# Second half of a hybrid recurrent layer: LRU's three buffers as slots of RWKV's values

## The chip, the cores and the metric

The kernel runs on one core of one Trainium2 chip, as one launch. The time is the device time of that launch in microseconds (us), lower is better. Each kernel is run several times and the median counts. Engines are named as in the profile: PE (TensorE matmul), PEld (its weight load), DVE (VectorE), ACT (ScalarE), POOL (GpSimd) and SP (SyncE, which issues DMAs here). POOL issues DMAs too.

## What is computed

One layer (`DEPTH = 1`) of a recurrent trunk with `D_MODEL` 1024 is run on 1024 prompt tokens and on 8 single tokens that continue from given states. The reference, cut to what matters here:

```python
xn = _rmsnorm(x, norm1_g)
P = xn @ w_in                                   # one projection, columns split in three groups
o_r, S_r = _rwkv7(pm, ...)                      # A: 6 heads x 64, delta-rule matrix state
o_h, S_h = _hgrn2(ph, ...)                      # B: 6 heads x 64, gated matrix state
o_l, h_l, c_l = _rglru(pl, ...)                 # C: 256 channels, elementwise recurrence
mix = concatenate([o_r, o_h, o_l])
x = x + mix @ w_out
xn2 = _rmsnorm(x, norm2_g)
x = x + square(relu(xn2 @ mlp_w1)) @ mlp_w2
y = _rmsnorm(x, final_g)
# _rglru: causal convolution of width 4, two block-diagonal gates r and i,
# h_t = a_t h_{t-1} + sqrt(1 - a_t^2) (i_t x_t), output h * gelu(gate)
```

The outputs are y and the updated states of the three groups.

## The kernel before

**Tiles and halves.** Channels lie on the 128 partitions, tokens along the free dimension. The tokens are worked in two halves: `hf` 0 is tokens 0 to 511, `hf` 1 is tokens 512 to 1023 with the 8 sample tokens behind them. RWKV and HGRN have three channel tiles each (j = 0, 1, 2; two heads in a tile), LRU two (t = 0, 1). Dense products are made in three float32r matmuls for one (high times high, high times low, low times high), so an input column of 128 channels costs 24 matmuls of 512 tokens in the first half, and 24 of 256 and 24 of 264 in the second.

**Two kinds of work on PE.** PE's order is written by the program itself (`weave`, L106): a clock `now` that is modelled from matmul sizes picks the next piece. Six kinds of streams hold what depends on the recurrences: `rw_chain`, `rw_inverse` (twice), `rw_operands`, `rw_finish`, `hgrn` and `lru`. The filler holds the dense work: the input columns (`projections`, in the order of `ORDER`, L44), then the output projection of the first half (`out_proj(0)`), that of the second half and the start of the MLP. A stream that is ready goes first; the filler is taken in pieces of two matmuls while no stream is ready. A piece that yields a key waits until that key is set, with a modelled delay. The other engines are ordered by a scheduler with priorities. Every engine then runs its list strictly in order, with semaphores between the engines.

**Names in the rows.** A name ends in its tile and its half. `in2944_1_0` is input column 2944 in the second half, from its token 0; columns 2944 and 3200 are LRU's x and gate branch for t = 0, columns 3072 and 3328 the same for t = 1. `out3_0` is row tile 3 of the output projection of the first half, `out0_512` row tile 0 of the second half. `ch` is RWKV's chain over chunks, `W`/`Y` its triangular inverse, `gram`, `hS`, `ho`, `hoT` are HGRN's products, `hsrow`, `hso`, `hsq` those of HGRN's sample tokens, `lg` LRU's gates. `x_2_1` is tile 2 in the second half.

**Slots.** Values wait for their stream in slots. RWKV's r, k and v are tiles of tag `pm` (6 slots, `RPM`), three of them per tile j. HGRN's four inputs are tiles of tag `hpm` (8 slots, `HPM`), and LRU's x branch (`xb`) and gate branch (`gl`) are tiles of `hpm` as well. LRU has a third buffer `gq` of tag `lq` with one slot, and its convolution output `lxc` lies in a tag `xc` with one slot. A counter `free` stands in for the slots in the modelled order: `take("hpm")` (L398) makes the filler wait until one is free. HGRN gives its four back at the end of `hg_run`, in the second half behind `hg_sample`; LRU gives its two back at the end of `lru` (L1207); RWKV gives its three back when the second quarter of `rw_operands` is done.

In the second half the filler's order is w0 r0 h0 r1 r2 h1 h2 l0 l1. With h1 and h2 taken all 8 `hpm` slots are held, so l0 (t = 0) stands still until tile 1 of HGRN has been through `hg_sample`, whose last product is `hsq1`.

**`lru(t, hf)`** (L1144) does the GELU factor of the gate (L1155 to L1159, in `gq` and `gl`), the convolution (L1165 to L1170, from `xb` to `lxc`), the gate products `lg` on PE with a Tanh on ACT (L1187), then exponentials (L1192, L1193), a square root on ACT behind a table load (L1199), the scan (L1202), the sample tokens' update (L1204, L1205) and the output (L1206). It writes r over `xb` and i over `gq`, so that L1204 is the last reader of `xb`.

**`out_proj`** (L1231): residual inputs `xr` are brought by a DMA on POOL's queue (L1260) into slots of `pm`, and the squares for the second norm (`sq`, L1251) use `pm` slots too. Weights of a column are brought twice: by SP into `raw` (one slot), from which ACT makes `wh` (L291) and a negated copy in `wl` (L295), upon which POOL adds the weights again by an accumulating DMA (L296). `wh` and `wl` have two slots each, so that a column's weights can be made once the column two before it is done. For columns in a list `SOON` DVE subtracts instead (L293); row tiles 0 and 1 of `out_proj(0)` are in it.

Of the kernel before, what the change touches and what calls it, by code (L numbers as in the profile page):

```python
# [9 lines left out]
F32 = mybir.dt.float32  # L10
# [7 lines left out]
P = 128  # L18
# [6 lines left out]
CH = ((0, 512), (512, 256), (768, 264))  # L25
HT = 512
HW = HT + NB
# [9 lines left out]
RPM, HPM = 6, 8  # L37
# [15 lines left out]
def kernel(ctx: ExitStack, tc: tile.TileContext, i, o):  # L53
# [49 lines left out]
    def ev(key, delay=1.5):  # L103
        done[key] = now[0] + delay
# [91 lines left out]
    def vec(name, k, n=1):  # L196
        return vt[:, at[name] + k:at[name] + k + n]
# [121 lines left out]
    rwp = phase1.enter_context(tc.tile_pool(name="rwp", bufs=1))  # L319
    phase0 = ExitStack()  # L320
    hgp = phase0.enter_context(tc.tile_pool(name="hgp", bufs=1, side="right"))
# [74 lines left out]
    free = {"pm": RPM, "hpm": HPM}  # L396

    def take(tag):  # L398

        yield lambda: free[tag] > 0  # L400
        free[tag] -= 1
# [25 lines left out]
    def take_out(hf, out, pt):  # L427

        if hf == 0:
            V.tensor_tensor(out, pt, rb0, op=ALU.mult)  # L430
        else:
            S.copy(out, pt)
# [16 lines left out]

    bnd = const.tile([P, 11], F32, name="bnd")  # L450

    def shifted(hf, col, name, out, tag, bufs):

        k = col // P
        pr = rwp.tile([P, HT + 16], F32, tag="praw", name=f"praw_{name}", bufs=1)
        pm = rwp.tile([P, HW], F32, tag=tag, name=f"pm_{name}", bufs=bufs)

        def evac(pt, c0, n):
            take_out(hf, pr[:, c0:c0 + n], pt)

        yield from in_proj(hf, col, evac, shift=True)
        mu = vec("mu", k)
        n = HT if hf == 0 else HW
        G.tensor_scalar(pm[:, :n], pr[:, :n], omm[:, k:k + 1], 0.0, op0=ALU.mult, op1=ALU.add)
        V.scalar_tensor_tensor(pm[:, 1:HT], pr[:, 0:HT - 1], mu, pm[:, 1:HT], op0=ALU.mult, op1=ALU.add)
        if hf == 0:
            G.tensor_copy(bnd[:, k:k + 1], pr[:, HT - 1:HT])
        else:
            V.scalar_tensor_tensor(pm[:, 0:1], bnd[:, k:k + 1], mu, pm[:, 0:1], op0=ALU.mult, op1=ALU.add)
            V.scalar_tensor_tensor(pm[:, HT:HW], pr[:, HW:HW + NB], mu, pm[:, HT:HW], op0=ALU.mult, op1=ALU.add)  # L470
        out.append(pm)
# [416 lines left out]
    hgin, lruin = {}, {}  # L888

    def hp_tile(name):  # L890
        return hgp.tile([P, HW + 3], F32, tag="hpm", name=name, bufs=HPM)
# [237 lines left out]
    def lru_proj(t, hf):  # L1129
        if hf == 1:  # L1130
            yield ("LRU", t, 0)
        x = []
        for w in ("xb", "gl"):
            yield from take("hpm")
            x.append(hp_tile(f"l{w}{t}_{hf}"))
        xb, gl = x
        G.tensor_copy(xb[:, 0:3], lcar[:, t, 0:3])
        yield from in_proj(hf, COL_LX + t * P, lambda pt, c0, n: take_out(hf, xb[:, 3 + c0:3 + c0 + n], pt))

        yield from in_proj(hf, COL_LG + t * P, lambda pt, c0, n: take_out(hf, gl[:, c0:c0 + n], pt))  # L1140
        lruin[t, hf] = x
        ev(("lru", t, hf), 1.5)

    def lru(t, hf):  # L1144
        yield ("lru", t, hf)
        xb, gl = lruin[t, hf]
        gq = hgp.tile([P, HW], F32, tag="lq", name=f"lq{t}_{hf}", bufs=1)
        n = HT if hf == 0 else HW
        s0 = hf * HT

        def f(ap):
            return ap[:, 0:n]
# [38 lines left out]
        m = gq  # L1191
# [12 lines left out]
            V.tensor_tensor(hs[:, HT:HW], rt[:, HT:HW], cst[:, t, 24:32], op=ALU.mult)  # L1204
            V.tensor_tensor(hs[:, HT:HW], hs[:, HT:HW], m[:, HT:HW], op=ALU.add)  # L1205
        V.scalar_tensor_tensor(mix[6 + t][:, s0:s0 + n], f(gl), 0.5, f(hs), op0=ALU.mult, op1=ALU.mult)  # L1206
        free["hpm"] += 2  # L1207
        ev(("LRU", t, hf), 14.0)
        if hf == 0:
            V.tensor_copy(lcar[:, t, 3:4], hs[:, HT - 1:HT])  # L1210
# [20 lines left out]
    def out_proj(hf):  # L1231
# [12 lines left out]
        def evac(m, c0, cn, pt, xt):  # L1244
            xm = x2[m][:, c0:c0 + cn]
            V.tensor_tensor(xm, pt[:, :cn], xt, op=ALU.add)
            a = acc[c0][:, :cn]
            if m == 0:
                act(a, xm, AF.Square)
            else:  # L1250
                sq = rwp.tile([P, HW], F32, tag="pm", name=f"sq{m}_{c0}", bufs=RPM)  # L1251
                act(sq[:, :cn], xm, AF.Square)
                V.tensor_tensor(a, a, sq[:, :cn], op=ALU.add)
            if m == KT - 1:
                ev(("acc", c0), 2.5)

        def load(m):
            ws[m] = next_w(m + 1 < lead or m >= lead)
            xts[m] = rwp.tile([P, HW], F32, tag="pm", name=f"xr{m}_{hf}", bufs=RPM)
            nc.gpsimd.dma_start(xts[m][:, :n], i["xt"][m * P:(m + 1) * P, s0:s0 + n])  # L1260

        yield from split(KS[:6])
# [14 lines left out]
        xts = {}  # L1277
# [148 lines left out]
        return tuple(nhl(k, c0, n))  # L1426

    def norms():
        yield from norm2(*CH[0], lambda nm: rwp.tile([P, HW], F32, tag="pm", name=nm, bufs=RPM))
        for c in CH[1:]:  # L1430
            yield from norm2(*c, lambda nm: mlps[0].tile([P, 512], F32, tag="wl4", name=nm, bufs=2))

# [73 lines left out]
    for m in range(KT):  # L1506
        if m < 6:
            tag = ("wh8", "wl8", "raw8", "wl8", "wh8", "last")[m]
            w = (mlp if m == 5 else wpool).tile([P, 2, FB, P], F32R, tag=tag, name=f"w2_{m}", bufs=2 if tag[0] == "w" else 1)
# [94 lines left out]
```

## Time and profile before

| | |
|---|---|
| median of 3 runs | 1579.41 us (1573.84 to 1581.77) |
| the profiled execution's own time | 1583.56 us |
| its span | 1581.8 us (1.76 us lie around it) |
| PE busy | 1500.9 us, 95% of the span |
| DVE, ACT, POOL busy | 757.3, 665.3, 382.5 us |
| granted TensorE clock, mean | 0.972 |
| moved by DMA | 146.98 MB, 93 GB/s |

The page gives one profiled execution. Busy shares are averages over stages: the streams end at about 760 us of the span, and what follows is dense work alone. Three stretches of it, PE's busy time and granted clock: up to 600 us 559.61 of 599 us at 0.97; 600 to 800 us 175.59 of 200 us at 0.91; from 800 us on 765.72 of 780 us at 0.99. Starts of instructions are given in us from the start of the span. A matmul in float32 that is no float32r shows as two records, and a matmul's own duration is longer than the distance to the next, since they are pipelined: distances of starts are what a row of matmuls costs.

### The profile page before, as it was taken

The numbers are of one execution on the slowest core, as the hardware profiler recorded it, in microseconds if no ns is written. First come the engines' busy times: TensorE is split into PE (matmuls) and PEld (weight loads), VectorE is DVE, ScalarE is ACT, GpSimd is POOL, SyncE is SP. The second block draws the span as 40 slices with busy tenths as digits, with TensorE's granted clock in tenths as the row PEclk, the third lists the DMA queues.
The fourth block names the chain that finished last, engine by engine and source line by source line (L and its number), as shares of the span: only waits on it lengthen the run. The fifth ranks groups of instructions, "written<-read, shape, count | busy, mean of one in ns | idle before, by whom it ended". The sixth has DMA issues, their size and how long they took to land.

```text
span 1581.8 us, 31488 instructions
## 1 busy us (share of the span) xinstructions
PE 1500.9 (95%) x13112; PEld 1322.7 (84%) x13112; DVE 757.3 (48%) x1799; ACT 665.3 (42%) x1433; POOL 382.5 (24%) x531
## 2 busy tenths in 40 slices
PE   8989999999998899978999999999999999999997
PEld 6767777888898888866798899889898989988887
DVE  7777866756566665574555222222222222222224
ACT  4544656546544556255434324232332323233232
POOL 4553323224335324323312110101111010101011
PEclk9989999998999999799999999999999999999999
DMA  4334334344434334235442544535344454544242
GB/s 152 125 68 96 84 81 94 79 83 98 91 75 96 74 81 91 62 73 124 119 128 81 107 80 99 102 83 104 83 104 83 102 92 85 102 86 101 47 93 108
DMA packets 53086, 146.98 MB, mean 93 GB/s; under 512 B 6960, under 2 KB 7248, under 8 KB 52944
## 3 DMA queue, kind: packets, MB, share of 16 engines
q0 software_dynamic: 22976, 65.33, 24.9%
q1 hardware_dynamic: 29824, 79.61, 16.1%
q8 instruction: 103, 1.69, 0.5%
q14 instruction: 39, 0.32, 0.1%
q10 hardware_dynamic: 144, 0.04, 0.0%
HBM read 138.87 MB, written 6.07 MB: 92 GB/s over the span
## 4 chain that ended last, share of the span: by engine, by line
PE 72%; DVE 10%; issue 6%; ACT 5%; DMA 4%; POOL 2%; POOLq 0%; SPq 0%; DVEq 0%; ACTq 0%
PE up L76 22%; PE dn L76 19%; PE in L76 13%; PE out L76 4%; PE ch L76 2%; PE W L76 2%; PE Y L76 2%; PE sc L76 1%; PE gram L76 1%; DMA wl_out<-in_w_out 1%; DVE rq L1035 1%; PE ho L76 1%; DMA raw_in<-in_w_in 1%; DMA wl_w<-in_w 1%; ACT gsq L768 1%
## 5 line engine op out<-in xcount | busy, mean ns | idle before, releaser
L76 PE MATMUL in<-xl,wh_in 128*128 128x512 f32 (+3 forms) x648 | 223.4, 345 | 2.1 <-DVE xl L385 2.1
L76 PE MATMUL in<-xh,wh_in 128*128 128x512 f32 (+3 forms) x648 | 223.9, 345 | 0.0
L76 PE MATMUL dn<-hh,wl_w 128*128 128x264 f32 (+2 forms) x696 | 223.2, 321 | 0.3 <-DMA wl_w<-in_w 0.2
L76 PE MATMUL dn<-hh,wh_w 128*128 128x264 f32 (+2 forms) x696 | 222.8, 320 | 0.0
L76 PE MATMUL dn<-hl,wh_w 128*128 128x264 f32 (+2 forms) x696 | 222.7, 320 | 0.0
L76 PE MATMUL in<-xh,wl_in 128*128 128x512 f32 (+3 forms) x648 | 221.4, 342 | 0.5 <-DVE wl_in L293 0.3
L1492 DVE TENSOR_TENSOR mix<-mix,dn 128x512 f32<-128x512 f32 (+2 forms) x192 | 98.4, 512 | 243.4 <-PE dn L76 243.4
L296 POOL DMA_DIRECT2D wl_w<-in_w x86 | 75.2, 877 | 575.4 <-ACT hh L1422 305.9
L291 ACT ACTIVATE wh_w<-raw_w 128x512 fp32r<-128x512 f32 (+1 forms) x90 | 70.7, 785 | 281.6 <-PE dn L76 228.0
L1421 DVE SCALAR_TENSOR_TENSOR rl<-up,rl 128x512 f32<-128x512 f32 (+2 forms) x96 | 49.5, 516 | 204.5 <-ACT rl L1420 204.4
L76 PE MATMUL up<-nxh,wh_w 128*128 128x264 f32 (+1 forms) x512 | 145.9, 285 | 0.1
L76 PE MATMUL up<-nxl,wh_w 128*128 128x264 f32 (+1 forms) x512 | 145.0, 283 | 0.5 <-POOL nxl L1318 0.5
L76 PE MATMUL up<-nxh,wl_w 128*128 128x264 f32 (+1 forms) x512 | 145.3, 284 | 0.0
L76 PEld LDWEIGHTS dn<-hh,wl_w 128*128 128x128 f32 x696 | 130.8, 188 | 14.1 <-DMA wl_w<-in_w 4.4
L76 PEld LDWEIGHTS dn<-hl,wh_w 128*128 128x128 f32 x696 | 130.9, 188 | 10.1
L76 PEld LDWEIGHTS dn<-hh,wh_w 128*128 128x128 f32 x696 | 131.0, 188 | 9.3
L76 PEld LDWEIGHTS in<-xl,wh_in 128*128 128x128 f32 x648 | 127.4, 197 | 13.4 <-DVE xl L385 4.2
L76 PEld LDWEIGHTS in<-xh,wl_in 128*128 128x128 f32 x648 | 127.1, 196 | 11.1 <-issue 1.0
L76 PEld LDWEIGHTS in<-xh,wh_in 128*128 128x128 f32 x648 | 127.3, 196 | 10.6 <-issue 0.7
L1420 ACT ACTIVATE rl<-up 128x512 f32<-128x512 f32 (+2 forms) x96 | 43.3, 451 | 141.0 <-PE up L76 140.9
L76 PE MATMUL up<-nl,wh_w 128*128 128x512 f32 x256 | 101.5, 397 | 0.0
L76 PE MATMUL up<-nh,wl_w 128*128 128x512 f32 x256 | 101.5, 396 | 0.0
(461 smaller groups left out, 3328.3 us busy)
## 6 DMA issues: line engine op xcount, KB each, us to landing
raw_in<-in_w_in SPq DMA_DIRECT2D x53, 512.0 KB, 3.4
wl_in<-in_w_in POOLq DMA_DIRECT2D x43, 512.0 KB, 5.7
raw_w<-in_w SPq DMA_DIRECT2D x32, 512.0 KB, 3.5
raw_w<-in_w SPq DMA_DIRECT2D x64, 256.0 KB, 2.7
wl_w<-in_w POOLq DMA_DIRECT2D x58, 256.0 KB, 4.1
wl_w<-in_w POOLq DMA_DIRECT2D x28, 512.0 KB, 5.6
raw_out<-in_w_out SPq DMA_DIRECT2D x16, 512.0 KB, 3.5
out_y_prompt<-yt SPq DMA_DIRECT2D x16, 256.0 KB, 2.0
```

The costliest lines, as they stand in the source:

```text
L76: PE.matmul(out, lhsT, rhs, start=start, stop=stop)
L291: act(wh[:, ks], raw[:, ks], AF.Copy)
L296: G.dma_start(wl[:, ks], src[:, ks], accum_op=ALU.add)
L768: act(sq, raw[:, g * 64:(g + 1) * 64], AF.Square, bias=sums[:, 0, g:g + 1], accum_out=sums[:, 1, g:g + 1])
L1035: V.tensor_tensor(qp[g][hp, h, :], qef[hp, gc], q[hp, gc], op=ALU.mult)
L1420: act(rl[:, :n], pt[:, :n], AF.Relu)
L1421: V.scalar_tensor_tensor(rl[:, :n], pt[:, :n], 0.0, rl[:, :n], op0=ALU.max, op1=ALU.mult)
L1492: V.tensor_tensor(x2[m][:, c0:c0 + n], x2[m][:, c0:c0 + n], pt[:, :n], op=ALU.add)
```

## The change

In the second half LRU's buffers become tiles of `pm`, three instead of two: `gq` is taken together with `xb` and `gl` in `lru_proj`, and all three are given back at the end of `lru`. In the first half all three are `hpm` slots (three instead of two with the tag `lq` beside them). The tag `lq` is gone. `pm` tiles are 3 columns wider (523 instead of 520), since `xb` holds 3 tokens of carry. What sets the filler free for l0 in the second half is thus RWKV's tile 1 rather than HGRN's tile 1.

```diff
+    def pm_tile(name):
+        return rwp.tile([P, HW + 3], F32, tag="pm", name=name, bufs=RPM)
+
...
-        pm = rwp.tile([P, HW], F32, tag=tag, name=f"pm_{name}", bufs=bufs)
+        pm = pm_tile(f"pm_{name}") if tag == "pm" else rwp.tile([P, HW], F32, tag=tag, name=f"pm_{name}", bufs=bufs)
...
         x = []
-        for w in ("xb", "gl"):
-            yield from take("hpm")
-            x.append(hp_tile(f"l{w}{t}_{hf}"))
-        xb, gl = x
+
+        for w in ("xb", "gl", "gq"):
+            yield from take("pm" if hf else "hpm")
+            x.append((pm_tile if hf else hp_tile)(f"l{w}{t}_{hf}"))
+        xb, gl, gq = x
...
-        xb, gl = lruin[t, hf]
-        gq = hgp.tile([P, HW], F32, tag="lq", name=f"lq{t}_{hf}", bufs=1)
+        xb, gl, gq = lruin[t, hf]
...
-        free["hpm"] += 2
+        free["pm" if hf else "hpm"] += 3
...
-            xts[m] = rwp.tile([P, HW], F32, tag="pm", name=f"xr{m}_{hf}", bufs=RPM)
+            xts[m] = pm_tile(f"xr{m}_{hf}")
```

Lines behind L451 move on by 3 or 4 in the numbering (L1200 becomes L1203, L974 becomes L977). The number of instructions on each engine is the same. PE's order is the same up to the place shown first; from there to `out1_512`, a row tile of the second half's output projection, it differs. Buffer numbers stand behind the names.

PE before, the end of the last HGRN column (`in2816`) in the second half and what comes next:

```order
L76 MATMUL in2816_1_256_7845<-xl7_3310,wh_in2816_1_7576 128x264
L76 MATMUL in2816_1_256_7845<-xh7_3302,wl_in2816_1_7577 128x264
L76 MATMUL W2_2_1_1_7959<-xm_2_1_1_7737,sa_2_1_1_7735 64x64 x8
L76 MATMUL W2_2_1_1_7959<-vr_2_1_1_7462,kt_2_1_1_7461 64x64 x8
L76 MATMUL ho_1_1_7978<-vt_1_1_7200,att_1_1_7198 64x64 x16
```

PE after, the same place:

```order
L76 MATMUL in2816_1_256_7845<-xh7_3302,wl_in2816_1_7577 128x264
L76 MATMUL in2944_1_0_7969<-xh0_3295,wh_in2944_1_7797 128x256
L76 MATMUL in2944_1_0_7969<-xl0_3303,wh_in2944_1_7797 128x256
L76 MATMUL in2944_1_0_7969<-xh0_3295,wl_in2944_1_7798 128x256
L76 MATMUL in2944_1_0_7969<-xh1_3296,wh_in2944_1_7797 128x256
L76 MATMUL W2_2_1_1_7975<-xm_2_1_1_7737,sa_2_1_1_7735 64x64 x8
L76 MATMUL W2_2_1_1_7975<-vr_2_1_1_7462,kt_2_1_1_7461 64x64 x8
```

LRU's first column now begins here; before, only stream work stands from here on.

PE before, the last product of HGRN's tile 1 (`hsq1`), behind which the dense work goes on:

```order
L76 MATMUL gate_1_1_1_8170<-pm_xg1_3608,gup_162 128x256
L76 MATMUL hso1_8173<-hq1_1_6529,hsst1_8120 64x1 x16
L76 MATMUL W5_2_1_1_8194<-xm_2_1_1_7737,sa_2_1_1_7735 32x32 x8
L76 MATMUL hsq1_8205<-hssq1_8191,bones_84 128x8
L76 MATMUL in2944_1_0_8242<-xh0_3295,wh_in2944_1_7797 128x256
```

PE after, the same product:

```order
L76 MATMUL hso1_8266<-hq1_1_6529,hsst1_8170 64x1 x16
L76 MATMUL W5_2_1_1_8287<-xm_2_1_1_7737,sa_2_1_1_7735 32x32 x8
L76 MATMUL in3200_1_0_8209<-xl7_3310,wh_in3200_1_7963 128x256
L76 MATMUL in3200_1_0_8209<-xh7_3302,wl_in3200_1_7964 128x256
L76 MATMUL in3200_1_256_8301<-xh0_3295,wh_in3200_1_7963 128x264
L76 MATMUL in3200_1_256_8301<-xl0_3303,wh_in3200_1_7963 128x264
L76 MATMUL hsq1_8304<-hssq1_8284,bones_84 128x8
L76 MATMUL in3200_1_256_8301<-xh0_3295,wl_in3200_1_7964 128x264
```

At `hsq1` none of LRU's 192 input matmuls stood in front before, and 74 stand in front now. The same count at later products: at `hqk_2_1` 126 before and 190 now; at `hsq2`, the last stream product of all, 156 matmuls of `out_proj(0)` before (of 192), and all 192 with 10 of `out0_512` now.

DVE before, around HGRN's subtraction for level 3 of tile 2 (`kq3_2_1`); the end of LRU's t = 0 (L1200 to L1206) stands 28 rows further on, behind the subtraction for level 5:

```order
L1242 TENSOR_TENSOR ml2_8757<-mix2_71,mh2_8749 128x512
L1242 TENSOR_TENSOR ml3_8758<-mix3_72,mh3_8750 128x512
L992 COPY_PREDICATED att_2_1_8494<-cmask_88,gram1_0_2_1_8700 128x64x2
L974 TENSOR_TENSOR kq3_2_1_8787<-b_2_1_8491 128x512
L992 COPY_PREDICATED att_2_1_8494<-cmask_88,gram1_1_2_1_8701 128x64x2
```

DVE after, the same subtraction:

```order
L1249 TENSOR_TENSOR mix0_69<-out0_0_8694,xr0_0_8692 128x512
L727 TENSOR_TENSOR rh0_2_1_1_8799<-ch_2_1_1_8785,mv_2_1_1_7738 128x64
L1203 SCALAR_TENSOR_TENSOR lgq0_1_7960<-lgq0_1_7960,lxc0_1_8416 128x520
L731 COPY mv_2_1_1_7738<-ch_2_1_1_8785 128x64
L1205 SCALAR_TENSOR_TENSOR lxc0_1_8416<-lxb0_1_7958,lcar_202,lgq0_1_7960 128x512
L1207 TENSOR_TENSOR lxc0_1_8416<-lxb0_1_7958,lcst_206 128x8
L1159 TENSOR_SCALAR lgq1_1_8381<-lgq1_1_8381 128x520
L995 COPY_PREDICATED att_2_1_8579<-cmask_88,gram1_0_2_1_8835 128x64x2
L977 TENSOR_TENSOR kq3_2_1_8885<-b_2_1_8576 128x512
```

The end of LRU's t = 0 now stands in front of level 3 of HGRN and of a step of RWKV's chain (`mv`). On POOL the DMA of `xr1_0` moves from before `in2304` to between `kq2_2_1` and `kq3_2_1`: its slot is the one that `lxb0_1` had.

More of the change, by code (lines that the diff above doesn't have):

```diff
@@ L1250, in evac @@
             else:
-                sq = rwp.tile([P, HW], F32, tag="pm", name=f"sq{m}_{c0}", bufs=RPM)
+                sq = pm_tile(f"sq{m}_{c0}")
                 act(sq[:, :cn], xm, AF.Square)
@@ L1428, in norms @@
     def norms():
-        yield from norm2(*CH[0], lambda nm: rwp.tile([P, HW], F32, tag="pm", name=nm, bufs=RPM))
+        yield from norm2(*CH[0], pm_tile)
         for c in CH[1:]:
```

## The prediction

> **What bounds the kernel now.** I read the page first: the span, the busy time by engine and the shares of the chain that ended last.
>
> ```profile
> span 1581.8 us, 31488 instructions
> PE 1500.9 (95%) x13112; PEld 1322.7 (84%) x13112; DVE 757.3 (48%) x1799; ACT 665.3 (42%) x1433; POOL 382.5 (24%) x531
> PE 72%; DVE 10%; issue 6%; ACT 5%; DMA 4%; POOL 2%; POOLq 0%; SPq 0%; DVEq 0%; ACTq 0%
> ```
>
> PE is the bound: it is busy for 95% of the span, and 72% of the last chain runs on it. The change takes no matmul away. It can only give time where PE stands or where its clock is low, and behind the streams there is dense work alone, so that a microsecond won there should reach the end whole. So I looked for the place where the program's order departs, the end of the last HGRN column, and read PE's timeline there, at the last matmul of that column, the first stream product behind it, and the place where input columns go on.
>
> ```profile
> 620.40 0.28 PE L76 MATMUL in<-xh,wl_in 128*128 128x264 f32 x1
> 620.61 0.27 PE L76 MATMUL W<-xm,sa 64*64 64x64 f32 x2
> 643.01 0.36 PE L76 MATMUL hsq<-hssq,bones 128*128 128x8 f32 x1
> 643.23 0.56 PE L76 MATMUL in<-xh,wh_in 128*128 128x256 f32 x1
> ```
>
> From 620.6 to 643.2 us, 22.6 us, there is no input matmul: a hole in the dense work, with streams alone. Then a table of windows by stage, cut at the hole, at the changes of the granted clock and at LRU's gate products. Its columns are the stretch, its length, busy time and instructions of PE, PEld, DVE, ACT and POOL, the clock, the DMA share and GB/s.
>
> ```profile
> 620.60:632.20 11.60, 8.46 (x203) 7.56 (x202) 6.47 (x21) 8.67 (x42) 6.86 (x11) 1.00 0.54 124
> 632.20:643.20 11.00, 9.77 (x94) 7.53 (x95) 5.10 (x16) 0.65 (x3) 4.62 (x7) 0.50 0.06 25
> 643.20:652.70 9.50, 9.50 (x57) 9.21 (x58) 4.23 (x15) 0.61 (x2) 4.72 (x5) 0.50 0.10 29
> 652.70:665.40 12.70, 12.16 (x111) 10.63 (x111) 8.53 (x23) 3.29 (x5) 3.00 (x7) 1.00 0.46 104
> 665.40:686.60 21.20, 20.16 (x248) 19.00 (x247) 13.93 (x37) 15.03 (x41) 5.29 (x6) 1.00 0.31 76
> 686.60:713.10 26.50, 17.94 (x163) 13.05 (x161) 21.19 (x52) 14.59 (x24) 7.34 (x10) 0.89 0.29 71
> 713.10:770.60 57.50, 50.29 (x386) 39.36 (x385) 28.27 (x62) 28.37 (x66) 19.67 (x25) 0.96 0.59 144
> ```
>
> Two things show. PE is busy for 18.23 of the hole's 22.6 us, but the second half of that is at half clock, and so are the first 9.5 us of dense work behind it. And from 686.6 to 713.1 it is DVE that is busy (21.19 of 26.5), with PE at 17.94. Last, the view of waits, for the hole (617 to 646 us, the first two rows, its longest) and for the stage behind it (643 to 770 us, the other rows): who waits, for whom, total, times, longest.
>
> ```profile
> PE hoT L81 <- DVE gs L765: 1.6, 1, 1.6
> PE W L76 <- DVE rh L724: 1.4, 1, 1.4
> ...
> PE lg L76 <- DVE lxc L1168: 6.0, 1, 6.0
> PE out L76 <- DMA wl_out<-in_w_out: 3.1, 2, 2.0
> PE ho L76 <- DVE hst L1060: 1.8, 3, 0.9
> PE ho L76 <- ACT ad L1051: 1.1, 1, 1.1
> ```
>
> In the hole PE never waits longer than 1.6 us in a piece. The one long wait is at 711 us: LRU's gate products wait 6.0 us for the convolution on DVE.
>
> **The change part by part.** *The hole is filled.* With three slots of RWKV's values at hand, LRU's columns no longer wait for HGRN's tile 1, and 74 of their matmuls stand in front of `hsq1`. What fits in? The stream work of the hole costs 8.46 us where the clock was full and 9.77 at half clock, which I halve to 4.9: 13.35 us at full clock. That leaves 22.6 - 13.35 = 9.25 us for dense work, if the streams keep their pace. The check goes from the other side, by the distance of dense matmuls of the same column, at half clock and behind it at full clock:
>
> ```profile
> 650.64 0.42 PE L76 MATMUL in<-xh,wh_in 128*128 128x264 f32 x1
> 651.30 0.42 PE L76 MATMUL in<-xh,wh_in 128*128 128x264 f32 x1
> 652.87 0.29 PE L76 MATMUL in<-xh,wh_in 128*128 128x264 f32 x1
> 654.60 0.28 PE L76 MATMUL in<-xh,wl_in 128*128 128x264 f32 x1
> ```
>
> From 652.87 to 654.60 lie 14 steps, 0.124 us each; from 650.64 to 651.30 three, 0.22 each. 74 x 0.124 = 9.15 us, which is what is free. I take 9.25. The bound from below is what stands idle with the clock as it is: 22.6 - 18.23 = 4.4 us. **First term: -9.25 (at least -4.4).**
>
> *The half clock behind the hole.* The 9.5 us from 643.2 to 652.7 are dense work at 0.50. If it is the thin work of the hole that brings the clock down, then with dense matmuls among the stream products it stays up, and the same work takes 4.75. **Second term: -4.75 (between 0 and -4.75).** The row for it is the table's second: PE was busy for 8.46 of 11.6 us with small products of heads, and then the clock fell. [...]
>
> *The weights in the hole.* LRU's first column has to have its weights when the hole begins. The accumulating DMAs that finish them are issued by POOL here; behind them is the page's row for such DMAs (count, size, median us from issue to landing):
>
> ```profile
> 614.77 0.92 POOL L296 DMA_DIRECT2D wl_in<-in_w_in  x1 [1.92 <-ACT hg L911]
> 624.10 0.91 POOL L296 DMA_DIRECT2D wl_in<-in_w_in  x1 [2.83 <-ACT wl_in L295]
> wl_in<-in_w_in POOLq DMA_DIRECT2D x43, 512.0 KB, 5.7
> ```
>
> The first lands at about 614.77 + 5.7 = 620.5, just as it is wanted, the second at 629.8, where half of the hole's dense work is still the first column's. So they are covered; were they not, the wait would be the 5.7 us of one landing at most. Term: 0.
>
> *LRU's end moves ahead of HGRN's level 3 on DVE.* This is what the change adds. DVE before has the subtraction for `kq3_2_1` at 686.28, and LRU's end for t = 0 far behind it; now that end (from the scan's factor to the sample tokens) stands in front of the subtraction, of the copies of `gram1` and of RWKV's `mv`, all of which are queued behind it, and PE's next HGRN products behind these. The first instruction of that end waits for ACT:
>
> ```profile
> 686.28 0.73 DVE L974 TENSOR_TENSOR kq<-b 128x512 f32<-128x512 f32 x1
> 687.54 0.72 POOL L979 TENSOR_TENSOR kq<-kq,hf 128x256 f32<-128x256 f32 x1 [4.72 <-ACT kq L975]
> 698.52 1.05 ACT L291 ACTIVATE wh_out<-raw_out 128x1024 fp32r<-128x1024 f32 x1
> 702.35 0.64 ACT L1199 ACTIVATE lq<-lq 128x520 f32<-128x520 f32 x1
> 703.02 0.70 DVE L1200 SCALAR_TENSOR_TENSOR lq<-lq,lxc 128x520 f32<-128x520 f32 x1 [2.50 <-ACT lq L1199]
> 705.36 0.14 DVE L1204 TENSOR_TENSOR lxc<-lxb,lcst 128x8 f32<-128x8 f32 x1
> ```
>
> DVE waits 2.50 us there for the square root, which stands on ACT behind a weight copy and a table load. Before, that wait held little; now HGRN's tile 2 and RWKV's chain are behind it. I take those 2.5 us whole. From the good side the cost is 0: LRU as a whole is earlier, and the wait may be over. From the bad side it is the distance from where level 3 was to where LRU's end was, 705.36 + 0.14 - 686.28 = 19.2 us. I lean to the near row, because LRU's columns come forward by some 14 us and take their end with them. **Third term: +2.5 (0 to +19.2).**
>
> *The DMA of `xr1`.* It takes the slot of `lxb0_1` and so waits, on POOL's queue, for the same end of LRU; `kq3_2_1`'s product on POOL, at 687.54 before, stands behind it. Its releaser is the one of the third term, and what is queued behind it is held on DVE by it too: nothing on top, or with LRU late, the same 19.2.
>
> *The rest.* `lxb` and `lgl` in wider tiles, the first half's third `hpm` slot, and the slot that `lq` leaves change no instruction of the first half nor its order: 0. LRU's t = 1 has its gate buffer in the slot that `xr0` uses as well, and its convolution still has the one `lxc` slot: no wait for these shows before, and I take 0 here and price it as a rival.
>
> *The sum.* -9.25 - 4.75 + 2.5 = -11.5 us. The profiled execution's own time is 1583.56 us, 4.15 above the median of 1579.41: 1572.1 against the one, **1567.9 us** on the median, which I predict. A check from the far end: suppose nothing at all makes the streams end earlier, and `hsq2` stays where it is.
>
> ```profile
> 758.23 0.28 PE L76 MATMUL hsq<-hssq,bones 128*128 128x8 f32 x2
> 758.37 0.48 PE L76 MATMUL out<-mh,wh_out 128*128 128x512 f32 x1
> 761.24 0.39 PE L76 MATMUL out<-mh,wh_out 128*128 128x512 f32 x1
> 763.83 0.50 PE L76 MATMUL out<-mh,wl_out 128*128 128x512 f32 x1 [1.96 <-DMA wl_out<-in_w_out]
> 770.59 0.28 PE L76 MATMUL out<-mh,wh_out 128*128 128x256 f32 x1
> ```
>
> Then 36 matmuls of `out_proj(0)` at 0.23 us (12 steps between the second and the third row, 2.87 us) and 10 of `out0_512` at about 0.12 lie ahead of it that lay behind: 8.3 + 1.2 = 9.5 us, and 11.5 with the wait of 1.96 for weights among them. The same size comes out of both ends.
>
> **The rivals.**
> *The clock stays low.* What brings the clock down may be something other than the hole's thin work. Then the second term is gone and the first is its lower bound: -4.4, 1575.0 us. For it: the dense 9.5 us from 643.2 ran at 0.50 too, so that dense work alone did not bring the clock back at once. Against it: the other long stretches, 652.7 to 686.6, are dense among streams and at 1.00. [...]
>
> *LRU's second tile waits.* PE's 6.0 us for the convolution come back for t = 1, whose convolution stands behind t = 0's output and whose first square stands behind `out0`: -11.5 + 6.0 = -5.5, 1573.9 us. For it: DVE is the fullest engine there (21.19 of 26.5). Against it: the view of waits has that wait once, not twice.
>
> *Slower.* LRU's end keeps its own time, because its gates wait for DVE and ACT rather than for its columns. Level 3 of tile 2 then goes from 686.28 to 705.5, 19.2 us later, in place of the 2.5, and the end of the streams with it: -14.0 + 19.2 = +5.2. PE runs out of dense work meanwhile, since all of `out_proj(0)` lies ahead, and a second hole costs a second stretch at half clock, 4.75: +9.95, 1589.4 us. It decides once L1207 (L1204 before) ends later than 686.28 + 14.0 = 700.3 us, which is 5.2 before it ended. For it: the 6.0 us wait and the full DVE just there. Against it: the columns that LRU waits for were the last thing to come, from 643.2 on.
>
> *More than the hole.* What the order makes wait goes too, since streams and dense work now lie beside each other up to the end: the 6.0, the 3.1 for weights, 1.8 and 1.1 of `ho`, 12.0 in all, and no third term: -14.0 - 12.0 = -26.0, 1553.4 us. For it: each of these has dense work that could stand ahead of it. Against it: the order puts LRU's gates as close behind their columns as before.
>
> That the change does nothing is excluded by PE's order, in which LRU's columns stand in the hole.
>
> **How the numbers follow.** The forecast has 0.48; its own range, with the second term between its bounds and the third between 0 and 2.5, goes from -14.0 to -6.75, 1565.4 to 1572.7 us. The low clock has 0.10, the second tile's wait 0.10, slower 0.17, more than the hole 0.15. About 0.5%, 7.9 us, is what a measurement of this kernel can tell from no change, so faster begins below 1571.5: the forecast but for 0.03, and the case of more, 0.60. Slower begins above 1587.3: the slower rival where the second half clock comes with it, 0.14. Within lie the low clock, the second tile, 0.03 of the forecast and 0.03 of the slower case without the clock, 0.26. The range goes from 1554 to 1584, near the bottom of the case of more and short of the slower rival with its clock; it leaves out 0.05 below and 0.14 above.
>
> **What would show it.** First term: input matmuls from 620.6 on, 70 or so ahead of `hsq1`, and `hsq1` still near 643. Second: a granted clock near 1.00 from 632 to 653. Together: the first dense matmul of `out0`, at 686.6 before, near 673. Third: DVE's wait at L1203 for ACT at 2.5 us or less, and level 3's subtraction (L977) no later than 700. The sum: `out0_512`, at 770.6 before, near 759. The forecast is wrong if the clock is low in the same place, if level 3 comes later than 700.3, or if PE shows a wait of over 5 us at 620 to 640 for weights.

## The result, and the profile after

The changed kernel took 1569.05 us in the median of 6 runs, the kernel before 1578.24 us in 6: a ratio of 0.995, with a 95% interval from 0.9926 to 0.9973. That is 9.2 us faster; timed again beside the experiments it was 10.6 us faster (0.9942, 0.9922 to 0.9963). The profiled execution took 1567.39 us with a span of 1565.4. Ratios and intervals leave out one run, of a variant below (the one with 1567.25 us in the median), that took 2032.54 us at a granted clock of 0.65.

The two profiled executions lie 16.2 us apart, more than the medians, and the first thing is to find where. The last matmul of the last HGRN column (`in2816`), where the two orders part, starts at 620.40 us before and at 617.41 after: 3.0 us were won ahead of the place at which the change begins, in code whose order is the same. They are no part of the change: two further profiles of the kernel before have that matmul at 617.90 and 617.02. From there to the last matmul of `out7_768` (826.06 and 811.23) it is 205.7 against 193.8 us, 11.8 less, and 1.3 more come behind. So the stage between these two matmuls is what has to be compared, and its times below count from the end of `in2816`.

The page after, with the busy times and the chain that ended last:

```profile
span 1565.4 us, 31493 instructions
PE 1484.2 (95%) x13112; PEld 1309.8 (84%) x13112; DVE 759.7 (49%) x1799; ACT 664.3 (42%) x1433; POOL 382.2 (24%) x531
...
PE 68%; DVE 12%; ACT 6%; DMA 6%; issue 5%; POOL 2%; SPq 0%; POOLq 0%; ACTq 0%; DVEq 0%
```

PE has the same number of matmuls and is busy for 16.7 us less over the whole span: much of what this pair of profiles shows is matmuls that ran at a higher clock (0.983 granted in the mean over the span, 0.972 before). In the stage itself PE is busy for 172.3 us and was for 179.8, 7.5 less, and idle for 4.4 less. PE's timeline after at the places that the prediction named:

```profile
617.41 0.28 PE L76 MATMUL in<-xh,wl_in 128*128 128x264 f32 x1
617.54 0.28 PE L76 MATMUL in<-xh,wh_in 128*128 128x256 f32 x1
...
642.31 0.39 PE L76 MATMUL hsq<-hssq,bones 128*128 128x8 f32 x2
...
669.02 0.39 PE L76 MATMUL out<-mh,wh_out 128*128 128x512 f32 x1
...
752.17 0.28 PE L76 MATMUL out<-mh,wh_out 128*128 128x256 f32 x1
...
811.23 0.28 PE L76 MATMUL out<-mh,wl_out 128*128 128x264 f32 x1
```

LRU's first column follows upon `in2816` at once. `out0` begins 51.6 us behind the end of `in2816`, 66.2 before; `out0_512` 134.8 against 150.2. The windows at the same four times as before, with the work 3.0 us further on in them:

```profile
620.60:632.20 11.60, 11.15 (x191) 10.45 (x188) 5.12 (x16) 5.97 (x38) 6.97 (x9) 1.00 0.48 118
632.20:643.20 11.00, 10.33 (x135) 8.87 (x133) 8.62 (x23) 3.44 (x7) 5.17 (x7) 1.00 0.51 121
643.20:652.70 9.50, 9.50 (x88) 8.84 (x87) 6.52 (x19) 3.82 (x6) 6.34 (x8) 1.00 0.44 103
652.70:665.40 12.70, 12.45 (x115) 11.09 (x113) 9.74 (x27) 7.49 (x16) 3.58 (x5) 1.00 0.41 111
```

The clock is at 1.00 in all four, and PE is idle for 1.1 of the first 22.6 us where it was idle for 4.4. A long wait of LRU's gates behind the hole is still there (643 to 757 us):

```profile
PE lg L76 <- DVE lxc L1171: 5.1, 1, 5.1
PE out L76 <- DMA wl_out<-in_w_out: 4.9, 2, 2.7
PE ch L76 <- DVE rh L727: 2.4, 1, 2.4
PE hsq L76 <- DVE hssq L1118: 1.7, 1, 1.7
```

And on DVE, the end of LRU's t = 0 with level 3 of HGRN's tile 2 behind it:

```profile
681.00 0.70 DVE L1203 SCALAR_TENSOR_TENSOR lgq<-lgq,lxc 128x520 f32<-128x520 f32 x1 [1.05 <-ACT lgq L1202]
...
682.94 0.14 DVE L1207 TENSOR_TENSOR lxc<-lxb,lcst 128x8 f32<-128x8 f32 x1
...
683.57 0.72 DVE L977 TENSOR_TENSOR kq<-b 128x512 f32<-128x512 f32 x1
```

DVE waits 1.05 us for the square root, and LRU's end is over at 65.7 us behind `in2816`, where it was over at 85.1 before.

### The profile page after: what moved, and what is told of

The parts are those of the page before. It is cut to its first block, busy times and chain, and to the rows that moved or that the text cites. A ratio compares the mean times of both kernels' runs of the same rounds, so it can differ in the third digit from the quotient of the medians.

```text
span 1565.4 us, 31493 instructions
## 1 busy us (share of the span) xinstructions
PE 1484.2 (95%) x13112; PEld 1309.8 (84%) x13112; DVE 759.7 (49%) x1799; ACT 664.3 (42%) x1433; POOL 382.2 (24%) x531
## 4 chain that ended last, share of the span: by engine, by line
PE 68%; DVE 12%; ACT 6%; DMA 6%; issue 5%; POOL 2%; SPq 0%; POOLq 0%; ACTq 0%; DVEq 0%
PE up L76 21%; PE dn L76 20%; PE in L76 12%; PE ch L76 2%; PE out L76 2%; PE W L76 2%; PE Y L76 2%; DMA raw_w<-in_w 1%; PE gram L76 1%; DMA wl_out<-in_w_out 1%; PE sc L76 1%; DMA wl_in<-in_w_in 1%; DMA raw_out<-in_w_out 1%; DMA mix<-in_xt 1%; PE ho L76 1%
## 5 line engine op out<-in xcount | busy, mean ns | idle before, releaser
L76 PE MATMUL in<-xl,wh_in 128*128 128x512 f32 (+3 forms) x648 | 218.8, 338 | 1.9 <-DVE xl L385 1.7
L76 PE MATMUL in<-xh,wh_in 128*128 128x512 f32 (+3 forms) x648 | 219.0, 338 | 0.0
L76 PEld LDWEIGHTS dn<-hh,wl_w 128*128 128x128 f32 x696 | 130.8, 188 | 13.7 <-DMA wl_w<-in_w 3.9
L76 PEld LDWEIGHTS in<-xl,wh_in 128*128 128x128 f32 x648 | 123.7, 191 | 13.0 <-DVE xl L385 4.2
L76 PEld LDWEIGHTS in<-xh,wl_in 128*128 128x128 f32 x648 | 123.6, 191 | 12.5 <-DVE wl_in L293 1.9
L76 PEld LDWEIGHTS in<-xh,wh_in 128*128 128x128 f32 x648 | 123.5, 191 | 10.4 <-issue 0.7
L76 PE MATMUL up<-nh,wh_w 128*128 128x512 f32 x256 | 101.5, 396 | 0.0
```

Of the source, the lines that this page charges most:

```text
L76: PE.matmul(out, lhsT, rhs, start=start, stop=stop)
```

## The experiments

Two theories were at stake. The one: the hole is filled with dense work, and the clock stays up with it. The other: something else that came with the new slots (a gate buffer of its own for each LRU tile, less waiting for slots) moves LRU along. Later a third question came up, whether the gain is partly given back where the streams end. In each experiment the ratio is to the kernel before, run beside it on the same chip.

**The slots without the early start.**

```diff
         if hf == 1:
             yield ("LRU", t, 0)
         x = []
+        if hf == 1:
+            yield lambda: free["hpm"] > 0
```

> The changed kernel with all its slots, but in the second half LRU's first column is held back until HGRN's tile 1 has given its slots back, so that PE's order is that of the kernel before, row for row. Theory (the hole is filled, and the clock with it): nothing is left of the gain, 1578 us within 4, ratio 0.998 to 1.002, with 22.6 us free of input matmuls and a stretch of 10 to 20 us at half clock in them. Rival (the slots themselves: a gate buffer of its own for each LRU tile lets LRU flow): half of the gain or more is kept, 1573.5 us or less.

Measured: 1583.15 us against 1580.23, ratio 1.0022 (1.0004 to 1.0041). Nothing of the gain is left, and the slots alone are rather a small loss. The hole and its half clock are back. The two rows are the stretch from the end of `in2816` to `out0`, and from there to the end of the stage; the columns are length, then PE's busy time, and the clock is the first number behind the five engines:

```profile
616.80:683.20 66.40, 60.09 (x709) 53.95 (x708) 38.65 (x112) 28.51 (x93) 25.28 (x33) 0.85 0.32 78
683.20:826.30 143.10, 120.61 (x950) 103.31 (x949) 81.94 (x168) 62.80 (x122) 37.66 (x47) 0.94 0.43 112
```

A clock of 0.85 over 66.4 us means 20 us at half clock. Here and before these come in one piece of 20.5 us that begins in the hole. The rival falls: it is the early start that carries the gain. What LRU's earlier end alone is worth in it was not tried.

**Matmuls of no use in the hole.** The product is read by nobody; nothing of the computation is left out.

```diff
         if hf == 1:
             yield ("LRU", t, 0)
         x = []
+        if (t, hf) == (0, 1):
+            pd = ps("big", "dum")
+            while free["hpm"] == 0:
+                for _ in range(2):
+                    mm(pd[:, 0:264], xh[0][:, 0:P], xh[1][:, 0:264])
+                yield 0.0
```

> The kernel before, with 72 matmuls of 264 columns put in the hole whose product nobody reads; LRU's columns start where they did. It does no useful work in the hole and only keeps PE busy. Theory: the granted clock is at 1.00 through the hole and behind it, which is worth the second term alone, 4.75 us: 1573.5 us, range 1571 to 1576. Rival (the clock is all of the gain): as the changed kernel, 1569 us. Rival (the half clock doesn't come from thin work): the clock stays at 0.50, the 72 cost 0.22 us each, 15.8 us against 4.4 us idle, and the time is 1578 to 1590 us.

Measured: 1578.31 us against 1580.23, ratio 0.9985 (0.997 to 1.0), a gain of some 2 us and not 4.75.

```profile
619.20:681.20 62.00, 60.03 (x780) 55.29 (x780) 38.20 (x111) 28.44 (x93) 24.85 (x33) 1.00 0.33 79
681.20:820.30 139.10, 118.11 (x949) 101.36 (x948) 81.47 (x168) 62.91 (x122) 37.39 (x46) 0.96 0.44 113
```

The clock is at 1.00 over the whole first stretch, where before had 0.85, so that the theory on its cause holds in this profile: with useless matmuls in the hole it stays up. The stretch is 4.2 us shorter than before (62.0 against 66.2), close to the second term. Further profiles of the kernel before, below, give a reason why the median shows only half of that.

**Two thirds of the dose.** Only the x branch of t = 0 starts early.

```diff
-            yield from take("pm" if hf else "hpm")
-            x.append((pm_tile if hf else hp_tile)(f"l{w}{t}_{hf}"))
+            tg = "pm" if hf and (t or w == "xb") else "hpm"
+            if (t, hf, w) == (0, 1, "gl"):
+                yield from in_proj(hf, COL_LX + t * P, lambda pt, c0, n: take_out(hf, x[0][:, 3 + c0:3 + c0 + n], pt))
+            yield from take(tg)
+            x.append((pm_tile if tg == "pm" else hp_tile)(f"l{w}{t}_{hf}"))
...
-        free["pm" if hf else "hpm"] += 3
+        if (t, hf) == (0, 1):
+            free["pm"] += 1
+            free["hpm"] += 2
+        else:
+            free["pm" if hf else "hpm"] += 3
```

> The changed kernel, but for t = 0 only the x branch takes a slot of RWKV's values; gate branch and gate buffer wait for HGRN's slots. 48 input matmuls instead of 74 stand in front of the last product of HGRN's tile 1. Theory: 48 x 0.124 = 5.95 us of the first term's 9.25; if the clock stays up as well, 9/14 of the gain or a little more is kept, some 6 to 7 us: 1571.5 us, range 1569.5 to 1573.5. Rival (a threshold: the clock falls as soon as the hole has any part without dense work): the first term's part alone and less, 3 us: 1575 us.

Measured: 1580.33 us, ratio 1.0011 (0.9995 to 1.0027). Both expectations missed: there is no gain at all. The windows are the filled part, the part that is left of the hole, and the dense work behind it:

```profile
619.20:634.30 15.10, 14.18 (x250) 13.13 (x249) 8.19 (x23) 9.13 (x44) 7.56 (x10) 1.00 0.41 95
634.30:644.70 10.40, 7.21 (x97) 5.56 (x95) 9.66 (x24) 2.72 (x5) 5.32 (x6) 0.80 0.54 128
644.70:654.30 9.60, 9.56 (x56) 9.27 (x57) 4.20 (x15) 0.72 (x3) 4.93 (x4) 0.50 0.10 27
```

A hole of 10.4 us is left; PE is idle for 3.2 of it, and the clock falls in it (0.80 in the mean) and stays down through the dense work behind (0.50), 13.7 us in all. So in this profile a shorter hole has the same consequence. That is the threshold rival's mechanism, at a price higher than it named. Not all of it is settled: in this one profile the stage takes 200.8 us, which is 4.8 less than in the profile of before, and over 12 executions nothing of that is left. PE also waits 7.6 us for the convolution of t = 1 here, 5.1 in the changed kernel, so that the clock need not be all of it.

**The changed kernel once more.**

> The changed kernel once more, for a second profile and a narrower interval beside the others. Theory: 1569 us within 2.5, the clock at 1.00 from 632 to 653 us, and part of the gain given back between the last product of HGRN's tile 2 and the third row tile of the second half's output projection, 2 to 4 us, because the streams' end moved less than the dense work. Rival (that part is where half-clock stretches happened to fall in the one profile): it is within 1 us of 0 in this profile.

Measured: 1569.67 us against 1580.23, ratio 0.9942 (0.9922 to 0.9963). The two rows are again the stretch to `out0` and the rest of the stage:

```profile
617.30:670.80 53.50, 50.90 (x638) 46.21 (x637) 36.33 (x99) 26.91 (x85) 23.32 (x31) 0.97 0.40 97
670.80:813.40 142.60, 123.48 (x1021) 106.90 (x1021) 86.98 (x181) 64.79 (x131) 39.08 (x49) 0.93 0.43 112
```

The stage takes 196.1 us, 9.6 less than before, where 12.7 had been won up to `out0`: 3.1 are given back behind it, of the size expected, though over a longer stretch than the expectation named. The clock is not at 1.00 all the way: 3.4 us at half clock came at 642.5.

**Is the part given back to be had?** Three kernels tried what might hold the streams' end. The first puts LRU's gates for t = 1 behind HGRN's last level; the second gives t = 1 a convolution slot of its own; the third, a control, makes the first edit in the kernel before.

```diff
             gram(l, *kq)
             kq = nx
+            ev(("gram", l, n), 0.0)
...
         yield D39
+        if (t, hf) == (1, 1):
+            yield ("gram", 5, "2_1")
```

> The changed kernel, but PE takes LRU's gate products for t = 1 only behind HGRN's last level (gram5) of tile 2, and dense work stands in their place. Theory (part of the gain is given back because PE's wait of 5.1 us for LRU's second convolution now stands ahead of HGRN's levels 3 to 5, so that the streams end as late as before): level 3 comes about 6 us earlier, the last stream product 3 us or more, and some 3 us come back: 1566.5 us, range 1565 to 1568. Rival (the dense work alone sets the end): as the changed kernel, 1569.7 us within 1.5. Rival (LRU's second tile is late for the output projection instead): 1572 us.

Measured: 1567.25 us against 1576.13, ratio 0.9941 (0.9921 to 0.9961): as the changed kernel. The time lies in the theory's range, but here the kernel before took 1576.13 us beside it where it took 1580.23 earlier, so that only the ratios can be compared. In its profile the wait for the convolution is gone, and yet level 3's subtraction comes 71.6 us behind `in2816` and the last stream product 141.5, no earlier than in the changed kernel's profiles (66.2 to 69.4, 139.0 to 142.5).

```diff
-        xc = hgp.tile([P, HW], F32, tag="xc", name=f"lxc{t}_{hf}", bufs=1)
+        xc = hgp.tile([P, HW], F32, tag="xcb" if (t, hf) == (1, 1) else "xc", name=f"lxc{t}_{hf}", bufs=1)
```

> The changed kernel with a slot of its own for the convolution output of LRU's t = 1 in the second half; PE's order is that of the changed kernel, and DVE makes the second convolution ahead of HGRN's tile 2 levels. Theory: PE's wait of 5.1 us for it goes (under 1 us is left), HGRN's levels 3 to 5 follow sooner, and 3 to 5 us are won: 1566 us. Rival (the wait goes but DVE's convolution pushes HGRN's levels 2 and 3 back by the same 4 us): as the changed kernel, 1569.7 us within 1.5.

Measured: 1567.99 us, ratio 0.9939 (0.9913 to 0.9965): as the changed kernel, and the last stream product comes at 141.9 us. The wait of 5.1 us for the convolution is gone from PE's list of waits, and the largest one for the gates is another:

```profile
PE out L76 <- DMA wl_out<-in_w_out: 5.2, 2, 2.7
PE lg L76 <- ACT lxb L1190: 2.5, 1, 2.5
```

> The kernel before with LRU's gate products for t = 1 behind HGRN's last level, as in the run of the changed kernel with the gates late. Here 36 matmuls of the first half's output projection still lie behind the last stream product, so that the streams' end isn't the bound. Theory: within 2 us of the kernel before, 1578 to 1582, though the longest wait there (6.0 us) shrinks or goes. Rival (that wait costs its 6.0 us wherever it stands): 1574 to 1575 us.

Measured: 1578.06 us against 1576.13, ratio 1.0009 (0.9987 to 1.003): nothing, as expected. But the edit did little here: the wait has only shrunk to 4.7 us, and the gates come 85.9 us behind `in2816`, where two further profiles of before have them at 83.9 and 84.0. So this control says little about the wait. In the changed kernel, taken away in two ways, it is worth nothing that these intervals show. A gain of up to 3 us isn't excluded by them, but none was found. My theory that the streams' end gives the 3 us back, through this wait, isn't borne out.

**More slots.** `RPM` is 7 instead of 6, and so `xr1` no longer waits for LRU's end.

```diff
-RPM, HPM = 6, 8
+RPM, HPM = 7, 8
```

> The changed kernel with 7 slots for RWKV's values instead of 6, so that the residual inputs of the output projection and LRU's second gate buffer wait less for LRU's buffers. PE's order is the same. Theory (the DMA of xr1 behind LRU's end costs nothing, as I took it): 1569.7 us within 1.5. Rival (POOL's queue held by that DMA delays HGRN's level 3): 2 to 4 us faster, 1566 to 1567.5.

Measured: 1568.3 us against 1576.13, ratio 0.9949 (0.9929 to 0.9969): no gain, although in the changed kernel POOL stands still for 3.10 us for that DMA:

```profile
683.38 0.57 POOL L1263 DMA_DIRECT2D xr<-in_xt  x1 [3.10 <-DVE lxc L1207]
```

**The kernel before, twice more.** The control above held a surprise in its profile: in the hole, in an order that is before's up to there, the clock was at half for 3.4 us and not for 20.5.

> The kernel before once more, for another profile of the stage from the last HGRN column's end to the first matmul of out0. In two profiles of this order of PE the hole had 20.5 us at half clock and the stage took 66.2 and 66.4 us, in a third (the kernel before with the gates late, the same order up to there) it had 3.4 us and took 59.5 us. Theory (the half clock in the hole depends on how the throttle's windows fall on the thin work, so that it comes in some executions): one of these two values, 66 or 59 to 60 us. Rival (it is always there in this kernel, and the third profile differs by its own change): 66 us again.

> As the look before it: 66 us with some 20 us at half clock, or 59 to 60 with under 7 us, by the theory; 66 again by the rival.

Measured: 59.4 and 59.5 us for the stretch, with 3.4 us at half clock in the hole, in executions of 1574.92 and 1572.61 us. The kernel before has two kinds of execution here, one with a long and one with a short stretch at half clock. The two stretches of the first of these profiles, the second of the kernel before:

```profile
617.90:677.30 59.40, 53.27 (x710) 47.66 (x709) 37.84 (x112) 28.47 (x93) 24.79 (x33) 0.97 0.34 83
677.30:816.90 139.60, 117.86 (x949) 100.99 (x949) 81.93 (x168) 63.15 (x122) 37.45 (x46) 0.96 0.42 113
```

In the first profiles of the two kernels the clock is at 1.00 or at 0.50, and from one change of it to the next it is always a multiple of 3.41 us; a window here is one such 3.4 us. In both kinds the same thing comes ahead of the fall, a window in which PE is busy for less than half, 1.61 and 1.60 us. First the profile of before that the prediction used, then its second profile, each from that window on:

```profile
628.80:632.20 3.40, 1.61 (x22) 1.26 (x22) 2.19 (x6) 1.76 (x8) 1.56 (x3) 1.00 0.34 115
632.20:635.60 3.40, 3.02 (x19) 1.90 (x20) 1.46 (x6) 0.37 (x1) 0.66 (x1) 0.50 0.01 2
635.60:642.50 6.90, 6.05 (x70) 5.00 (x69) 3.47 (x9) 0.00 (x0) 3.57 (x5) 0.50 0.10 38
642.50:652.70 10.20, 10.20 (x72) 9.85 (x67) 4.39 (x16) 0.89 (x3) 5.11 (x5) 0.50 0.09 27
```

```profile
626.40:629.80 3.40, 1.60 (x22) 1.26 (x22) 2.11 (x7) 1.76 (x8) 0.06 (x1) 1.00 0.33 112
629.80:633.20 3.40, 3.23 (x20) 2.10 (x20) 1.05 (x6) 0.37 (x1) 2.02 (x2) 0.50 0.03 7
633.20:638.00 4.80, 3.62 (x75) 2.91 (x74) 3.53 (x11) 0.07 (x1) 3.45 (x5) 1.00 0.14 55
638.00:650.00 12.00, 12.00 (x102) 10.86 (x103) 7.36 (x24) 3.11 (x6) 6.85 (x9) 1.00 0.26 71
```

In the second profile the clock is at 1.00 again after one window at half clock; in the first it is at 0.50 for six, in the last three of which PE is busy throughout (10.20 of 10.20 us). In the first window at half clock PE was busy for 3.23 us where the clock then came back and for 3.02 where it didn't, and the three other profiles of this order fall in with that (3.32 and 3.15 where it came back, 2.87 where not). But busy time alone doesn't decide it: in those last three windows half clock lasts on with PE busy throughout, and in the changed kernel's third profile, below, a second window at half clock follows one with PE busy for 3.40 of 3.40 us. Where the fall lies on the work hardly differs: counted from `in2816` the fall comes at 11.8 and 12.0 us in the two long cases, at 11.9, 12.0 and 12.1 in the short ones. What decides it isn't settled.

**The change for t = 0 alone.**

```diff
-            yield from take("pm" if hf else "hpm")
-            x.append((pm_tile if hf else hp_tile)(f"l{w}{t}_{hf}"))
+            yield from take("pm" if (t, hf) == (0, 1) else "hpm")
+            x.append((pm_tile if (t, hf) == (0, 1) else hp_tile)(f"l{w}{t}_{hf}"))
...
-        free["pm" if hf else "hpm"] += 3
+        free["pm" if (t, hf) == (0, 1) else "hpm"] += 3
```

> The change for LRU's t = 0 alone: its three buffers are slots of RWKV's values, t = 1 has three of HGRN's slots. PE's order is the changed kernel's, row for row, and DVE's and ACT's move by some rows. Theory (only the start of t = 0 matters, since it is what fills the hole): the whole gain, 1567 to 1570 us, ratio 0.993 to 0.996. Rival (t = 1's slots carry part of it): 2 us or more of it are lost, ratio over 0.9965.

Measured: 1568.52 us against 1580.79, ratio 0.9932 (0.9906 to 0.9958): the whole gain. The slots of t = 1 have no part in it that shows.

**The changed kernel, a third profile.**

> The changed kernel once more, for another profile of the same stage. Five profiles with this order of PE in it took 51.6, 53.5, 54.7, 57.0 and 58.1 us with 0, 3.4, 6.8, 10.2 and 10.2 us at half clock. Theory: on that line, 51.6 plus 0.5 to 0.65 us for each microsecond at half clock. Rival (the half clock is not what parts these profiles): off it by over 2 us.

Measured: 54.9 us with 6.8 us at half clock, 0.2 from the profile of the kernel with more slots that had the same. The line gives 55.0 to 56.0, so it lies 0.1 below its edge and far inside the 2 us of the rival. The time was 1568.88 us.

```profile
617.90:672.80 54.90, 52.55 (x638) 47.71 (x637) 35.62 (x100) 26.77 (x85) 23.53 (x31) 0.94 0.38 94
672.80:812.10 139.30, 120.38 (x1021) 104.70 (x1020) 86.93 (x181) 64.69 (x131) 39.04 (x49) 0.95 0.44 115
```

None of the variants beats the changed kernel by more than their intervals.

## Why the prediction was right, and which step was not

**The sum over all profiles.** The stage took 205.7 and 209.4 us in the two profiles of before's order with the long half clock in the hole, 207.5 in the mean; 199.0, 198.6 and 199.6 in the three with a short one, 199.1; and 193.8, 196.1 and 194.2 in the three of the changed kernel, 194.7. So, by these few profiles, the change is worth 4.4 us in executions in which the clock would have come back at once, and 12.8 in those in which it would not. The measured 9.2 and 10.6 lie between. If these means hold, about two executions of three were of the second kind, (9.9 - 4.4) / (12.8 - 4.4); of the five profiles two were. The useless matmuls, with 201.2 us, are 6.3 better than the one kind and 2.1 worse than the other; two to one would make a gain of 3.5 us of that, against 1.9 between the medians, which is about what one to one makes. So the share is known only roughly.

The 4.4 can be read from the rows too. In the second profile of before, PE is idle for 6.1 us up to `out0` and 21.7 behind it (length less busy time), 27.9 together; after, in the third profile, for 2.3 and 18.9, 21.3. Some 6.6 us of idle time are gone. Against that the changed kernel has more time at half clock in the stage, 6.8 us up to `out0` and 13.7 behind it against 3.4 and 10.2, which at a clock of 0.50 costs up to 3.4 us, by estimate: -3.2. The two stages lie 4.8 apart, so that 1.6 are left unexplained.

**First term (-9.25).** Mis-sized. At nearly the same clock the stretch to `out0` went from 59.4 us to 53.5 (3.4 us at half clock in both): -5.9. The formula was right and its length wrong: I took 22.6 us of hole, which is what it lasts at half clock, and counted its stream work at full clock. At nearly full clock the hole itself is shorter, 20.1 us from `in2816` to `hsq1` in the second profile of before, 22.4 in the first. With the 13.35 us of stream work that leaves 6.75, not 9.25. The 74 matmuls, 9.2 us, do stand in the hole, as said, but they stretch it from 20.1 to 24.9 us, so that about 4.4 of them fit in and 4.8 set the streams back. "If the streams keep their pace" was the condition that failed. What I gave as the bound from below was 4.4 as well; that the whole stage shows the same number where the clock comes back at once is partly chance, since time at half clock goes into that.

**Second term (-4.75).** The mechanism holds: with dense matmuls in the hole the long half clock is gone, and with the useless ones as well: the clock is at 1.00 through the hole in the first profile after and in theirs. Its size is 66.3 - 59.4 = 6.9 us up to `out0`, of which 4.6 are the stretch behind the hole that I priced and 2.3 the hole's own length, which I had put into the first term. But it is there only in some executions of before: three of the five profiles of this order had the short one. And the changed kernel isn't free of it: in its three profiles 0, 3.4 and 6.8 us at half clock come in the stretch, now behind 640 us. The two terms together were 14.0 and this pair of profiles shows 14.6; over many executions it is less.

**Third term (+2.5).** It is there in its place, at about the size I gave. From level 2's subtraction of tile 2 on DVE to level 3's it takes 8.1 us in all three profiles of the changed kernel and 5.4 or 5.5 in the three of before. The two subtractions, in the second profile of before and in the first one after:

```profile
671.45 0.73 DVE L974 TENSOR_TENSOR kq<-b 128x512 f32<-128x512 f32 x1
676.89 0.73 DVE L974 TENSOR_TENSOR kq<-b 128x512 f32<-128x512 f32 x1
```

```profile
675.50 0.72 DVE L977 TENSOR_TENSOR kq<-b 128x512 f32<-128x512 f32 x1
683.57 0.72 DVE L977 TENSOR_TENSOR kq<-b 128x512 f32<-128x512 f32 x1
```

Between the second two stands the end of LRU's t = 0, with the 1.05 us of waiting for ACT; that it makes the 2.6 us more is read from DVE's order and was not tried by itself. That level 3 comes 66.2 us behind `in2816`, and 65.9 in the profile of before, hides this, because before's long half clock lies ahead of it there; in the two further profiles of before it comes at 59.0 and 59.1. So the streams are set back by 4.8 us at `hsq1`, by 7.1 or more at level 3, and at `hsq2` by 6 to 11 (139.0 to 142.5 against 131.5 and 133.0). How much of that reaches the end of the stage is open. Behind `out0` the stage takes 142.2, 142.6 and 139.3 us after, and 139.5, 139.6 and 139.1 before. The two long ones have 20.5 us at half clock there, the 139.3 has 13.7, and those of before have 13.7, 10.2 and 10.2. That the clock is the cause was not tried by itself.

**The terms at nothing.** The DMA of `xr1` does hold POOL, for 3.10 us, and costs nothing that the interval of the kernel with more slots shows. PE waits 0.6 us for weights in the hole. The slots of LRU's t = 1 have no part, as the change for t = 0 alone shows. But "no wait for these shows before" was a wrong reading: the wait of 6.0 us at 711 us is the one for the single slot of the convolution. DVE begins the convolution of t = 1 only behind the output of t = 0 (L1206), and PE's gates of t = 1 wait for it:

```profile
705.74 0.70 DVE L1206 SCALAR_TENSOR_TENSOR mix<-lgl,lxc 128x520 f32<-128x520 f32 x1
706.90 0.55 DVE L1165 TENSOR_SCALAR lxc<-lxb,vt 128x520 f32<-128x520 f32 x1
711.21 1.23 PE L76 MATMUL lg<-lxc,lruw 128*128 128x260 f32 x2 [5.96 <-DVE lxc L1168]
```

With a slot of its own it begins 45.0 us behind `in2816`, where the changed kernel has it at 71.1 to 74.3.

**The rivals.** *The clock stays low* named -4.4, which is the gain where the clock plays no part, but its mechanism, that thin work isn't the cause, is refuted by the useless matmuls, with which the clock was at 1.00. *LRU's second tile waits* and *more than the hole* both speak of the 6.0 us wait. It was t = 1's already before, so that it could not come back for t = 1; it stays, at 5.1, and taking it away changes nothing that shows. *Slower* fell, since L1207 ended at 65.7 us behind `in2816`, well inside its limit of 700.3 - 620.4 = 79.9. The check from the far end, 9.5 us of work moved ahead of `hsq2`, came nearest in its number, and by luck: `hsq2` stayed where it was (139.0 us behind `in2816` against 137.8) only against the profile with the long half clock, and against the two others of before it came 6 to 11 us later.

So the gain, 9.2 and 10.6 us for 11.5, came out well partly by luck. The first term was too large by 3. The second is 6.9 in one kind of execution and nothing in the other, about 4.6 in the mean if two executions of three have the long half clock, and that there are two kinds was no part of the prediction. The time, 1569.05 us for 1567.9, lies nearer still because the median of before that I started from, 1579.41, was 1.2 above that of all six runs.

## What to carry to other kernels

Where dense work runs out among thin dependent work, price the hole at the clock that it will have once it is filled, not at the length that the profile shows, and expect the thin work to be slowed by what fills it (`hsq1` came 4.8 us later behind `in2816`). Here a hole that was filled for two thirds gained nothing, and in its profile the clock still fell to 0.50 in the 10.4 us that were left of it. Before saying that a stream kept its place, compare it with a profile that has the same clock ahead of it. Take several profiles of the kernel before, ahead of reading a price from one: here one profile of it stood for only some of its executions, and the distance of two single profiles was 16 us where the medians lay 9 apart.

## What the runs showed of the hardware

In the first profiles of the two kernels the granted clock was 1.00 or 0.50, and from one change of it to the next it was always a multiple of 3.41 us. In this stage the stretches at half clock lasted 20.5, 6.8, 3.4 and 3.4 us before, and 3.4, 6.8, 3.4 and 6.8 us after; what the other profiles have at half clock in it, 3.4, 6.8, 10.2, 13.7 and 20.5 us up to `out0` or behind it, agrees with that. In the hole the clock fell without a long gap: in the 3.4 us ahead of the fall PE was busy for 1.6, and PE's longest wait there was 1.6 us; with matmuls of no use in the hole it stayed at 1.00. Nor was PE idle for half of a window ahead of every fall, by the profile's busy time: in the changed kernel's second and third profiles the clock fell behind 3.4 us in which PE was busy for 2.7 and 3.2, and at 365.9 us before and 366.7 after, far ahead of this stage, behind 3.4 us in which it was busy throughout. Its return was uneven: at the same work the clock came back after 3.4 us in three executions and after 20.5 in two.
